# Hybrid encoder block: row differences tied behind a copy, fill drawn earlier, weight sums in other columns

## The chip, the cores and the metric

The kernel runs on one core of a Trainium2 chip. The metric is device time in microseconds (us) of one execution, lower is better; the median of several runs is compared. A core has five engines that work side by side, each on its own queue in order: TensorE (PE in the profile; PEld is its weight load), VectorE (DVE), ScalarE (ACT), GpSimd (POOL) and SyncE (SP), which here issues nearly all DMA transfers. SBUF is the on-chip memory of 128 partitions, PSUM the accumulators that TensorE writes.

## The reference, cut to what matters

One layer of a streaming encoder, 1024 tokens of width 1024, float32. A normalised input is projected once; three mixers work on parts of the projection, their outputs are projected, gated and summed, and a gated MLP with a short convolution follows.

```python
u = rms_norm(x, norm_mix_g) @ w_in                   # parts for MLA, FoX, SSD, gates
y_a = mla_branch(u_mla, ...) @ w_br_mla              # 8 heads, chunk-causal softmax
y_b = fox_branch(u_fox, ...) @ w_br_fox              # 8 heads, softmax with decay
y_c = ssm_branch(u_ssm, ...) @ w_br_ssm              # conv, SSD scan, gated norm
g = sigmoid(u_gate + b_gate)
x = x + (g[0] * y_a + g[1] * y_b + g[2] * y_c) @ w_out
x = x + conv_ffn(rms_norm(x, norm_ffn_g), ...)       # silu(gate) * val, then @ ffn_w_down
# inside the SSD scan, per chunk
decay = where(causal, exp(a_cum[i] - a_cum[j]), 0)   # per head
cb = C @ B.T
y_diag = (cb * decay) @ xdt
states = B.T @ (decay_to_end * xdt);  y_off = C @ h_in * exp(a_cum)
```

## The kernel before, in words

Every float32 product is computed as three products of a high and a low part (`split`: ScalarE copies the high part, VectorE subtracts it to get the low part), in tiles of 128 by 128 by 512. The stages, in order: projections for MLA and FoX, then attention, then the SSD scan, then the three branch projections (FoX, MLA, SSM), the output projection, and the MLP.

**Fill.** The columns of `w_in` for the scan's convolution (12 blocks) and the gates (24 blocks) need nothing but the normalised input. They are not computed in a stage of their own but dealt out as fill: `all_fill` is a generator that issues a block's 48 matrix multiplies (two halves of 24) and yields after every `grain` triples, with a booked cost of 0.65 us a triple. `grain` is 2 in attention (steps of 6 multiplies) and 4 in the scan (steps of 12). Results that other engines have to take out of PSUM are scheduled behind it by a simulated clock, `later(us, fn)`.

**merge.** TensorE's order in attention and scan is written out by `merge(streams, fill_us)`. It gets generators, each with a booked cost, and always advances the one whose share of its cost is smallest. `fill_us` is the cost that the fill may spend in this call; what is not spent stays owed to the next call. In attention a unit is a pair of query tiles of one head, four units a head, 16 heads; unit n issues its scores (`cost_s`) beside the value products of unit n-2 (`cost_v`), with fill worth `FILL_ATT` (1.08) times their cost. For n < 2 there are no value products yet. Ahead of the scan stands `merge([], 6.0)`, fill alone; the scan's ten turns get `FILL_SSD`, 11.3 us in eight turns, 12.0 in the ninth and 24.5 in the tenth, or what is left of the fill.

**Scan.** A chunk of the kernel's scan is a tile of 128 tokens (c = 0 to 7). Turn c runs `ssd_a` of chunk c, `ssd_b` of c-1 and `ssd_c` of c-2. `ssd_a` transposes the inputs into PSUM (L1506, tag `tp`, two slots; copied by L1507), transposes B and multiplies C with B into another `tp` tile (L1517, L1519), and splits B's transposes: ScalarE's copy `bTh`, VectorE's `bTl`, then VectorE multiplies the product with the causal mask (`cbm`, L1522). For each quarter of four heads ScalarE forms row differences of the cumulated decays with Relu (L1538, four instructions of 128 by 128), one exponential (L1539), and VectorE multiplies with `cbm` (L1540) to `E`. `ssd_b` adds states, the diagonal products `py` from `E` (L1574) and the products with the incoming state, scales by the gate, squares, takes a root on POOL and scales the result on ScalarE (L1601, kept in `scaled`). `ssd_c` transposes it (L1609) and copies it (L1610) for the store `ys_d`.

**Branches.** For each branch b the operand is loaded (`ar`), split (`ah`, `al`), and for eight columns j a weight tile and a gate tile are loaded, the weight split, and `ybr` computed (L1729); `out_half` (L1666 to L1673) multiplies with the gate and sums. The first two FoX operands are loaded during the scan; their split is tied behind `scaled` of the last chunk. The last gate block's activation is tied behind the second operand's copy.

**Weight sums.** The MLP's down projection uses sums of quarters of its weight. `down_sums` takes one of 11 row blocks: it first issues the stores of the previous set (`down_flush`), then two loads of 512 KB, four POOL additions (L939 to L942), and leaves two stores of 512 KB for the next flush. Six sets are formed during the projections, five in the branch stage, in tiles that the branch stage also uses for the first FoX operands and, from column 4 of the second branch, for four operands of the third (`early_raw`).

**What sets the order.** TensorE's instructions stay in the order written inside `tc.manual_schedule`. The other queues are ordered when the program is built, by a scheduler that simulates the program and issues what is ready. Two things bind it: `keep_in_program_order` puts an instruction behind the one traced before it on its engine (the loads and stores of `down_sums` are so bound), and `behind_(a, b)` puts a behind b on the same engine:

```python
def behind_(ins, other):
    tc.add_manual_dep(ins.ins, other.ins.name,
                      mybir.DependencyInfo(mybir.DependencyClass.NoSync, ...))
    return ins
```

It is an order in the queue only, without a semaphore.

Of the kernel before, what the change touches and what calls it, by code (L numbers as in the profile page):

```python
# [15 lines left out]
AF = mybir.ActivationFunctionType  # L16
# [26 lines left out]
def block_kernel(ctx: ExitStack, tc: tile.TileContext, x, positions, norm_mix_g, w_in, b_gate,  # L43
# [1380 lines left out]
    with ExitStack() as pt__:  # L1424
        atp = pt__.enter_context(TP("atp", 2))
        psp = pt__.enter_context(TP("psa", 1, space=PSUM))
        a_pm = Ring(atp, [P, S], F32, "pm", 6)
        a_nmx, a_rs = (Ring(atp, [P, 4], F32, n, 4) for n in ("nmx", "rs"))
        a_th, a_tl = (Ring(atp, [P, 512], F32R, n, PVLAG + 2) for n in ("pth", "ptl"))
        a_o1 = Ring(atp, [64, 256], F32, "o1", 1)  # L1430
        a_o2 = Ring(atp, [64, 256], F32, "o2", 4)
        a_s = Ring(psp, [P, 512], F32, "s", 3)
        a_tp = Ring(psp, [P, 512], F32, "tp", 2)
        o_acc = psp.tile([P, 2, 256], F32, name="o", tag="o")
        with tc.manual_schedule(engines={mybir.EngineType.PE}):
            names = [(br, h) for br in range(2) for h in range(8)]
            merge([], 5.0)
            units = [(n, jp) for n in range(16) for jp in range(4)]
            heads = {0: load_head(atp, *names[0])}
            load_values(atp, heads[0])  # L1440
            done = []
            for n in range(len(units) + 2):
                st, share = [], 0.0
                if n < len(units):
                    hn_, jp = units[n]
                    if jp == 0 and hn_ + 1 < 16:
                        heads[hn_ + 1] = load_head(atp, *names[hn_ + 1])
                    if jp == 3 and hn_ + 1 < 16:
                        load_values(atp, heads[hn_ + 1])
                    pn = []  # L1450
                    done.append((heads[hn_], jp, pn))
                    share += cost_s(jp)
                    st.append((scores(heads[hn_], jp, pn), cost_s(jp, len(heads[hn_].passes))))
                if n >= 2:
                    share += cost_v(done[n - 2][1])
                    me = []
                    me.append(values(*done[n - 2], me))
                    tp_next[:] = me
                    st.append((me[0], cost_v(done[n - 2][1])))
                merge(st, FILL_ATT * share)  # L1460
            flush()
            while pend:
                run_pv()
                clk[0] += 0.44
                run_until(clk[0])
            run_until(clk[0] + 3.0)
# [7 lines left out]
    with ExitStack() as ps__:  # L1474
# [22 lines left out]
        def ssd_a(o, c):  # L1497

            if c + 1 < NT:
                load_bc(obj[c + 1], c + 1)  # L1500
                load_rows(obj[c + 1], c + 1)
            xT = pool.tile([P, D], F32, name=uid("xT"), tag="xT", bufs=1)
            for g in range(2):
                pt = psp.tile([P, 512], F32, name=uid("stp"), tag="tp", bufs=2)
                for j in range(4):
                    T.transpose(pt[:, j * P:j * P + P], o.xs[:, 4 * g + j, :], ident)  # L1506
                A.activation(xT[:, 512 * g:512 * g + 512], pt, AF.Copy)  # L1507
                yield 0.44
            yield 0.0
            if c + 1 < NT:  # L1510
                load_xs(obj[c + 1], c + 1)
            o.bT = [pool.tile([P, 2, P], F32R, name=uid(n), tag=n) for n in ("bTh", "bTl")]
            o.c_ = [pool.tile([P, 2, P], F32R, name=uid(n), tag=n) for n in ("Ch", "Cl")]
            cbm = pool.tile([P, 2, P], F32, name=uid("cbm"), tag="cbm")
            pt = psp.tile([P, 4, P], F32, name=uid("stp"), tag="tp", bufs=2)
            for g in range(2):
                T.transpose(pt[:, g, :], o.bc[:, g, :], ident)  # L1517
            for g in range(2):
                T.matmul(pt[:, 2 + g, :], o.bc[:, g, :], o.bc[:, 2 + g, :], start=True, stop=True)  # L1519
            split(*o.bT, pt[:, 0:2, :])  # L1520
            split(*o.c_, o.bc[:, 2:4, :])
            V.tensor_mul(cbm, pt[:, 2:4, :], tri.unsqueeze(1).to_broadcast([P, 2, P]))  # L1522
            xv = xT.rearrange("p (h d) -> p h d", d=64)
            o.xd = pool.tile([P, 16, 64], F32, name=uid("xd"), tag="xd")
            V.tensor_mul(o.xd, xv, hb(dt, c))
            o.xdd = [pool.tile([P, 16, 64], F32R, name=uid(n), tag=n, bufs=1) for n in ("xddh", "xddl")]
            xdd = pool.tile([P, 16, 64], F32, name=uid("xdd"), tag="xdd", bufs=1)
            if c + 1 < NT:
                G.tensor_mul(xdd, xv, hb(dend, c))
            o.y = pool.tile([P, 16, 64], F32, name=uid("y"), tag="y", bufs=3)  # L1530
            G.tensor_mul(o.y, xv, Db.unsqueeze(2).to_broadcast([P, 16, 64]))
            yield 0.65
            o.E = []
            for q in range(4):
                E = pool.tile([P, 4, P], F32, name=uid("E"), tag="E", bufs=4)
                for hh in range(4):
                    h = 4 * q + hh
                    A.activation(E[:, hh, :], o.row[:, h, :], AF.Relu, scale=-1.0, bias=cumc[:, c, h:h + 1])  # L1538
                A.activation(E, E, AF.Exp, scale=-1.0)  # L1539
                V.tensor_mul(E, E, cbm[:, q // 2:q // 2 + 1, :].to_broadcast([P, 4, P]))  # L1540
                o.E.append(E)
                if q == 1 and c + 1 < NT:
                    split(*o.xdd, xdd)
                yield 0.0
# [71 lines left out]
        with tc.manual_schedule(engines={mybir.EngineType.PE}):  # L1616
            obj = {c: Head() for c in range(NT)}
            load_bc(obj[0], 0)
            load_xs(obj[0], 0)
            load_rows(obj[0], 0)  # L1620
            merge([], 6.0)
            grain[0] = 4
            for c in range(NT + 2):
                st = []
                if c < NT:
                    st.append((ssd_a(obj[c], c), 1.6))
                if 0 <= c - 2 < NT:
                    st.append((ssd_c(obj[c - 2], c - 2), *((0.88, 0.6) if c <= NT else (8.0, 0.2))))
                if 0 <= c - 1 < NT:
                    st.append((ssd_b(obj[c - 1], c - 1, obj.get(c - 2)), 6.4, 0.05))  # L1630
                merge(st, FILL_SSD[c])
            for _ in range(4):
                if advance(fill) is None:
                    break
# [3 lines left out]
    with ExitStack() as pe_:  # L1638
# [39 lines left out]
        for b, wsrc, nk in ((1, w_br_fox, 4), (0, w_br_mla, 4), (2, w_br_ssm, 8)):  # L1678
# [26 lines left out]
                al.append(l)  # L1705
            wv = wsrc[0].rearrange("(k p) c -> p k c", p=P)
            for j in range(NK):
                if (b, j) in ((1, 4), (0, 0), (2, 1), (2, 3), (2, 5)):
                    down_sums(ws_tiles())
                elif (b, j) in ((0, 3), (2, 6)):  # L1710
                    down_flush()
                if (b, j) == (0, 4):
                    early_raw = [t.rearrange("p a s -> p (a s)") for t in ws_tiles()]
                    for k in range(4):
                        SY.dma_start(early_raw[k], ys_d[k])
                if b == 0 and j >= 4:
                    early.append(ssm_operand(j - 4, early_raw[j - 4]))
                wh, wl = load_w(fpl, wv[:, :, j * P:j * P + P], nk, (scaled, gate_behind)[j][0] if b == 1 and j < 2 else None)
                g = fpl.tile([P, S], F32, name=uid("gl"), tag="t4", bufs=4)
                SY.dma_start(g, g_d[b][j])  # L1720
                pss = [psp.tile([P, 512], F32, name=uid("ybr"), tag="half") for half in range(2)]
                parts = [(half, 0, nk) for half in range(2)]
                if j == 0:
                    parts = [(half, k, k + 1) for k in range(nk) for half in range(2)]
                for half, k0, k1 in parts:
                    hs = slice(512 * half, 512 * half + 512)
                    for k in range(k0, k1):
                        for i, (w_, a_) in enumerate(((wh, ah), (wh, al), (wl, ah))):
                            T.matmul(pss[half], w_[:, k, :], a_[k][:, hs], start=k == 0 and i == 0,  # L1729
                                     stop=k == nk - 1 and i == 2)  # L1730
                    if k1 == nk:
                        out_half(b, j, half, g, pss[half])
# [481 lines left out]
```

## Time and profile before

| | us |
|---|---|
| median of 3 runs | 2002.59 |
| lowest, highest | 2002.17, 2005.0 |
| profiled execution, its own time | 2003.73 |
| its span | 2002.0 |

| stretch of the span (us) | stage |
|---|---|
| 0 to 384 | projections, MLA and FoX heads |
| 384 to 902 | attention with fill |
| 903 to 1094 | scan with fill |
| 1094 to 1270 | branches: FoX to about 1138, MLA to about 1182, SSM |
| 1270 to 1363 | output projection |
| 1363 to 2002 | MLP |

How to read the rows: a row of a timeline has the start in us from the span's start, the length, engine, line, instruction, output and inputs, and in brackets the time that the engine sat idle before it and what released it. "issue" means that the profile shows no releaser. A row of waits has the engine and line that waited, what it waited for, total us, times and longest. A row of a window has the stretch, its length, the busy time of PE, PEld, DVE, ACT and POOL with the number of instructions, TensorE's granted clock (1.00 is full), the DMA engines' busy share and GB/s; a window of one line only has PE and PEld.

### The profile page before, as it was taken

To read this page: it belongs to the slowest core of one execution; us is meant where nothing else is said; L and a number is where in the kernel's file an instruction comes from. 1 tells how busy PE (TensorE), PEld (TensorE's weight loads), DVE (VectorE), ACT (ScalarE), POOL (GpSimd) and SP (SyncE) were. 2 spreads that over 40 slices of the span, in tenths; PEclk is the share of its full clock that TensorE was granted. 3 is DMA by queue.
4 is the path that set the end of the run, shared out by engine and by line. 5 is a ranking of instruction groups with operands and counts; after the bars stand their busy time and mean duration, and the time that the engine had idled before them with its cause. 6 is when DMAs were issued, how large, how long until landed. Compare 5 with 4: busy or idle time off the path is not lost.

```text
span 2002.0 us, 28702 instructions
## 1 busy us (share of the span) xinstructions
PE 1977.5 (99%) x10185; PEld 1676.7 (84%) x10185; DVE 1365.9 (68%) x2345; ACT 944.5 (47%) x1778; POOL 651.9 (33%) x636
## 2 busy tenths in 40 slices
PE   8999999999999999999999999999999999999998
PEld 7989888888888888888888888888888888888887
DVE  7777567267666677656885476568997777666665
ACT  5555323255555556557775132225454444544432
POOL 5133322021212223213331252100764544423764
PEclk9999999999999999999999999999999999999999
DMA  5166857543535444427654786433332211249575
GB/s 178 52 195 210 277 179 224 165 125 105 139 114 145 122 120 133 125 78 238 183 192 139 259 284 202 144 119 107 104 95 90 78 55 53 78 159 337 188 262 185
DMA packets 278265, 312.18 MB, mean 156 GB/s; under 512 B 19197, under 2 KB 209289, under 8 KB 278122
## 3 DMA queue, kind: packets, MB, share of 16 engines
q1 hardware_dynamic: 278120, 310.35, 49.6%
q8 instruction: 80, 1.31, 0.3%
q14 instruction: 63, 0.52, 0.1%
q10 hardware_dynamic: 2, 0.00, 0.0%
HBM read 217.17 MB, written 93.13 MB: 155 GB/s over the span
## 4 chain that ended last, share of the span: by engine, by line
PE 86%; DVE 4%; issue 3%; DMA 3%; POOL 2%; ACT 2%; SPq 1%; ACTq 0%; DVEq 0%; POOLq 0%
PE mm L1179 19%; PE fx L798 9%; PE dn L2161 8%; PE ybr L1729 7%; PE ua L1820 6%; PE uc L1820 5%; PE ud L1820 4%; PE wo L1865 4%; PE s L1296 4%; PE tp L1384 3%; PE ub L1820 2%; PE fxv L188 2%; PE py L1574 1%; PE o L1357 1%; PE ckv L517 1%
## 5 line engine op out<-in xcount | busy, mean ns | idle before, releaser
L1326 POOL TENSOR_SCALAR pm<-pm,rs 128x128 f32<-128x128 f32 (+7 forms) x128 | 105.3, 826 | 413.9 <-DVE rs L1325 290.1
L1179 PE MATMUL mm<-hnh,wh 128*128 128x512 f32 x576 | 236.9, 411 | 0.0
L1179 PE MATMUL mm<-hnh,wl 128*128 128x512 f32 x576 | 226.0, 392 | 0.0
L1179 PE MATMUL mm<-hnl,wh 128*128 128x512 f32 x576 | 225.8, 392 | 0.0
L2161 PE MATMUL dn<-dr,dr 128*128 128x512 f32 x592 | 182.3, 389 | 0.0
L1319 ACT ACTIVATE pm<-s,nmx 128x128 f32<-128x128 f32 (+2 forms) x192 | 110.4, 581 | 64.9 <-DVE nmx L1314 61.4
L2161 PEld LDWEIGHTS dn<-dr,dr 128*128 128x128 f32 x592 | 111.1, 188 | 23.0
L1179 PEld LDWEIGHTS mm<-hnh,wl 128*128 128x128 f32 x576 | 108.1, 188 | 24.6
L1179 PEld LDWEIGHTS mm<-hnl,wh 128*128 128x128 f32 x576 | 108.9, 189 | 15.6
L1179 PEld LDWEIGHTS mm<-hnh,wh 128*128 128x128 f32 x576 | 108.8, 189 | 15.5
L1390 DVE TENSOR_TENSOR ptl<-tp,pth 128x512 fp32r<-128x512 f32 (+1 forms) x160 | 98.4, 633 | 32.8 <-ACT pth L1389 30.7
L1389 ACT ACTIVATE pth<-tp 128x512 fp32r<-128x512 f32 (+1 forms) x160 | 84.8, 555 | 72.6 <-PE tp L1384 72.5
L2161 PE MATMUL dn<-dr 128*128 128x512 f32 x296 | 115.3, 389 | 1.1 <-DVE dY L2178 1.1
L135 DVE TENSOR_TENSOR dr<-dr,dr 128x1024 fp32r<-128x1024 f32 x52 | 75.8, 1465 | 49.1 <-ACT dr L134 47.2
L1729 PE MATMUL ybr<-ah,wl 128*128 128x512 f32 x256 | 99.7, 390 | 1.1 <-DVE wl L135 1.1
L1729 PE MATMUL ybr<-al,wh 128*128 128x512 f32 x256 | 99.8, 390 | 0.0
L1729 PE MATMUL ybr<-ah,wh 128*128 128x512 f32 x256 | 99.7, 389 | 0.0
L134 ACT ACTIVATE dr<-dr 128x1024 fp32r<-128x1024 f32 x52 | 55.1, 1061 | 73.0 <-PE dn L2161 50.0
L1312 DVE TENSOR_REDUCE nmx<-s 128x1 f32<-128x384 f32 (+3 forms) x128 | 65.8, 518 | 32.7 <-PE s L1296 19.1
L134 ACT ACTIVATE wh<-wr 128x1024 fp32r<-128x1024 f32 (+1 forms) x40 | 35.1, 877 | 98.1 <-PE ybr L1729 45.9
L1384 PE MATMUL tp<-ident,pm 128*128 128x128 f32 x576 | 79.8, 273 | 0.6 <-POOL pm L1326 0.6
L135 DVE TENSOR_TENSOR wl<-S,wh 128x1024 fp32r<-128x1024 f32 x42 | 63.2, 1504 | 23.3 <-ACT wh L134 23.3
(531 smaller groups left out, 5782.7 us busy)
## 6 DMA issues: line engine op xcount, KB each, us to landing
dr<-act_d SPq DMA_DIRECT2D x99, 256.0 KB
wr<-in_w_in_dram SPq DMA_DIRECT2D x36, 512.0 KB
g_d<-t SPq DMA_DIRECT2D x24, 512.0 KB
gl<-g_d SPq DMA_DIRECT2D x24, 512.0 KB
wr<-in_ffn_w_up_dram SPq DMA_DIRECT2D x23, 512.0 KB
ws<-in_ffn_w_down_dram SPq DMA_DIRECT2D x22, 512.0 KB
wsum_d<-ws SPq DMA_DIRECT2D x22, 512.0 KB
act_d<-fa SPq DMA_DIRECT2D x22, 512.0 KB
```

The source lines that it names most:

```text
L134: i = A.activation(h, src, AF.Copy) if he is A else he.tensor_copy(h, src)
L135: return i, le.tensor_sub(l, src, f32(h))
L798: T.matmul(p, a(k), b(k), start=k == 0 and i == 0, stop=k == NK - 1 and i == 2)
L1179: T.matmul(ps, a[:, k, :], b[half][:, k, :], start=(k == 0 and i == 0), stop=(k == NK - 1 and i == 2))
L1319: pss[cj][1][0] = later(t0 + 0.9 + 0.1 * cj, lambda cj=cj, a_=a_, b_=b_: A.activation(p_[:, a_:b_], pss[cj][0][:, :b_ - a_], AF.Exp, bias= ...
L1326: G.tensor_scalar(p_[:, 0:n * P], p_[:, 0:n * P], rs[:, 3:4], 0.0, op0=ALU.mult, op1=ALU.add)
L1384: T.transpose(pt[:, off:off + P], pn[qi][0][:, k * P:k * P + P], ident)
L1389: later(cs + 0.05, lambda th=th, pt=pt, off=off: A.activation(th[:, :off], pt[:, :off], AF.Copy))
L1390: pl[0] = later(cs + 0.6, lambda th=th, tl=tl, pt=pt, off=off: V.tensor_sub(tl[:, :off], pt[:, :off], f32(th[:, :off])))
L1729: T.matmul(pss[half], w_[:, k, :], a_[k][:, hs], start=k == 0 and i == 0, stop=k == nk - 1 and i == 2)
L1820: T.matmul(ps, a, b, start=first and n == 0, stop=n == 11, skip_group_check=not first)
L2161: T.matmul(ps[m], a[:, ts_], b[:, 512:], start=first_ and j == 0 and q == 0, stop=j == NFH - 1 and q == 2, skip_group_check=not first_)
```

## The change

Four edits. The first two units of attention draw 2.0 us more of fill each. The fill ahead of the scan is 9.0 us instead of 6.0. All 16 row differences of a scan chunk are tied on ScalarE behind the copy of that chunk's transposed B. The first set of weight sums in the branch stage moves from column 4 to column 2 of the FoX branch, the second from column 0 of the MLA branch to column 6 of the FoX branch, and the flush of the second set's stores from column 3 to column 2 of the MLA branch; the last three sets stay.

```diff
@@ attention, for n in range(len(units) + 2)
-                merge(st, FILL_ATT * share)
+                merge(st, FILL_ATT * share + (2.0 if n < 2 else 0.0))
@@ ssd_a
-            split(*o.bT, pt[:, 0:2, :])
+            b_copy, _ = split(*o.bT, pt[:, 0:2, :])
...
-                    A.activation(E[:, hh, :], o.row[:, h, :], AF.Relu, scale=-1.0, bias=cumc[:, c, h:h + 1])
+                    behind_(A.activation(E[:, hh, :], o.row[:, h, :], AF.Relu, scale=-1.0, bias=cumc[:, c, h:h + 1]),
+                            b_copy)
@@ ahead of the scan
-            merge([], 6.0)
+            merge([], 9.0)
             grain[0] = 4
@@ branches, for j in range(NK)
-                if (b, j) in ((1, 4), (0, 0), (2, 1), (2, 3), (2, 5)):
+                if (b, j) in ((1, 2), (1, 6), (2, 1), (2, 3), (2, 5)):
                     down_sums(ws_tiles())
-                elif (b, j) in ((0, 3), (2, 6)):
+                elif (b, j) in ((0, 2), (2, 6)):
                     down_flush()
```

## The prediction

> **What bounds the kernel now.** I read the page first, then TensorE's waits stage by stage, then the timelines of all engines around each wait. First the page: its head and the line of busy time.
>
> ```profile
> span 2002.0 us, 28702 instructions
> PE 1977.5 (99%) x10185; PEld 1676.7 (84%) x10185; DVE 1365.9 (68%) x2345; ACT 944.5 (47%) x1778; POOL 651.9 (33%) x636
> ```
>
> TensorE is busy for 1977.5 of 2002.0 us. The diff takes no matrix multiply away; it only changes their order and what runs beside them. So it can win only idle time of TensorE in the stages that it touches, and it can lose wherever it uncovers a latency. The waits of TensorE in attention and at its end are few (microseconds in total, times, longest):
>
> ```profile
> PE o L1349 <- DVE o L1367: 1.6, 1, 1.6
> PE stp L1506 <- DVE o L1367: 0.9, 1, 0.9
> PE s L1296 <- ACT pm L1319: 0.8, 1, 0.8
> PE tp L1384 <- POOL pm L1326: 0.6, 1, 0.6
> ```
>
> In the branch products there is one:
>
> ```profile
> PE ybr L1729 <- DVE wl L135: 1.1, 1, 1.1
> ```
>
> And in the scan three waits, as TensorE's timeline shows them (start, length, instruction, in brackets the idle time before it):
>
> ```profile
> 955.94 0.63 PE L1506 MATMUL stp<-ident,t 128*128 128x128 f32 x4 [1.16 <-issue]
> 999.11 0.63 PE L1506 MATMUL stp<-ident,t 128*128 128x128 f32 x4 [0.79 <-PE py L1574]
> 1020.34 0.63 PE L1506 MATMUL stp<-ident,t 128*128 128x128 f32 x4 [1.38 <-issue]
> ```
>
> That is 0.8 + 0.6 in the first heads, 0.9 where the scan's first transposes wait for attention's last PSUM read, 3.33 in the scan, 1.1 in the second branch: 6.7 us that the edits aim at. The 1.6 lies in the middle of attention, where no edit is. 0.2% of this kernel, about what a measurement of it can tell from no change, is 4 us.
>
> **The change, part by part.** *Fill at the start of attention.* No instruction is added. Two units draw 2.0 us more each from the fill, and the 1.4 us of waits above come a few units later. Their late partners are a score row's maximum and a normalisation, which the first convolution block's vector work holds up; that block now ends a unit sooner in program order, so its taps meet shorter score rows. Ends: -1.4 (both gone) and +1.6 (the shifted phase makes another wait like the row of 1.6). I take half of the gain, -0.7.
>
> *Fill before the scan, 9.0 for 6.0.* Twelve more multiplies (one step at the grain of the fill) can stand under the 0.9 us wait. Ends -0.9 and 0; 2.7 us of work over a wait of 0.9 is ample, so -0.9.
>
> *What both draws take from the end.* The fill is finite: 36 blocks of 48 multiplies, booked at 0.65 us for three, 374.4 us in all. Before, 5.0 are drawn first, 1.08 x 16 x 14.48 = 250.2 in attention (the two cost functions give 0.74 + 1.22 + 1.86 + 2.50 and 0.72 + 1.60 + 2.48 + 3.36 for a head's four units, 14.48 together), 6.0 before the scan and 11.3 x 8 + 12.0 in its first nine turns: 363.6. The tenth turn, which asks for 24.5, gets what is left, 10.8, in steps of twelve multiplies 48. The trace agrees: the 72 multiplies after the scan's last diagonal product are 24 of turn nine and 48 of turn ten.
>
> ```profile
> 1076.20:1094.00 17.80, 17.22 (x72) 13.13 (x72) 1.00 0.59 192
> ```
>
> After, 370.6 are drawn by then and 3.8 are left, one step of 12. So 36 multiplies that stood at the scan's end go earlier, and chunk 7's output chain loses its cover. TensorE's rows are transposes of chunk 6, twice of chunk 7, and the second branch multiply:
>
> ```profile
> 1081.70 0.60 PE L1609 MATMUL stp<-ident,y 128*128 128x128 f32 x4
> 1087.63 0.60 PE L1609 MATMUL stp<-ident,y 128*128 128x128 f32 x4
> 1090.85 0.60 PE L1609 MATMUL stp<-ident,y 128*128 128x128 f32 x4
> 1094.34 0.50 PE L1729 MATMUL ybr<-al,wh 128*128 128x512 f32 x1
> ```
>
> ScalarE's are the scaling of chunk 7, the second copy of its transposes and the first branch operands:
>
> ```profile
> 1082.96 1.15 ACT L1601 ACTIVATE y<-y,yr 128x1024 f32<-128x1024 f32 x1
> 1091.48 0.60 ACT L1610 ACTIVATE yT<-stp 128x512 f32<-128x512 f32 x1 [2.48 <-PE stp L1609]
> 1091.98 2.00 ACT L134 ACTIVATE ah<-ar 128x1024 fp32r<-128x1024 f32 x2
> ```
>
> Count from chunk 6's last transposes (1081.70 = 0). Four transposes and 12 multiplies take 1090.85 - 1087.63 = 3.22 us. By the row of 72 twelve multiplies are 12 x 17.22/72 = 2.87, so four transposes 0.35. After the change chunk 7's transposes start at 3.22 and, with nothing between, at 3.57; TensorE is free at 3.92. The scaling is done at 2.41 (1082.96 + 1.15), so the transposes do not wait. The second copy starts 0.63 after its transposes (1091.48 - 1090.85) and the first branch operand 0.50 after that: 4.70. Its low half lets the second branch multiply start 2.36 later (1094.34 - 1091.98): 7.06. One multiply (0.24) falls into the gap, so TensorE idles 7.06 - 0.24 - 3.92 = 2.9 us where it idled nothing. Ends: +1.0, if the operand's copy goes right behind the scaling (a little behind 2.41 instead of 4.70, with the first weights' copy between), and +3.5, if one more copy as long as the 0.60 of the row above slips in. I take +2.9, since the order in the rows above has the operand behind both copies.
>
> *The row differences behind the copy of B's transposes.* No instruction and no semaphore is added; 16 activations per chunk go behind one copy on ScalarE's queue, and behind them wait four exponentials, VectorE's four products, and TensorE's diagonal products. The three waits of 3.33 us are for the two-slot PSUM ring: the next chunk's transposes need the slot of B's transposes, which VectorE's mask product reads last. Chunk 2, then chunk 5:
>
> ```profile
> 949.25 0.61 PE L1519 MATMUL stp<-bc 128*128 128x128 f32 x4
> 944.34 1.26 ACT L1538 ACTIVATE E<-row,strict 128x128 f32<-128x128 f32 x4
> 945.51 0.58 ACT L1507 ACTIVATE xT<-stp 128x512 f32<-128x512 f32 x1
> 951.84 0.37 ACT L134 ACTIVATE bTh<-stp 128x256 fp32r<-128x256 f32 x1
> 955.43 0.41 DVE L1522 TENSOR_TENSOR cbm<-stp,tri 128x256 f32<-128x256 f32 x1
> 963.27 1.00 PE L1574 MATMUL py<-xd,E 128*128 128x64 f32 x8
> ...
> 992.77 0.61 PE L1519 MATMUL stp<-bc 128*128 128x128 f32 x4
> 993.49 0.37 ACT L134 ACTIVATE bTh<-stp 128x256 fp32r<-128x256 f32 x1
> 998.59 0.41 DVE L1522 TENSOR_TENSOR cbm<-stp,tri 128x256 f32<-128x256 f32 x1
> ```
>
> In chunk 2 B's copy comes 2.0 us after its transposes end at 949.86, and row differences at 944.34 push the copy that feeds VectorE to 945.51: with them gone both come over 1 us sooner, and the 1.16 us wait goes. In chunk 5 the copy is already prompt, and VectorE comes to the mask product only 5 us later; the tie helps there only if VectorE's order changes too. So I count the first wait whole and the other two by half: -(1.16 + 1.08) = -2.25. Ends: -3.33, and a loss from this side: between B's transposes and the first diagonal product ScalarE and VectorE have this much to do (window, span, then busy time of PE, PEld, DVE, ACT, POOL):
>
> ```profile
> 949.90:963.30 13.40, 12.24 (x67) 10.31 (x66) 12.91 (x19) 9.65 (x21) 2.81 (x4) 1.00 0.67 195
> L1538 ACT ACTIVATE E<-row,strict 128x128 f32<-128x128 f32 x112 | 35.7, 390 | 11.6 <-PE py L1574 11.3
> L1539 ACT ACTIVATE E<-E 128x512 f32<-128x512 f32 x28 | 17.1, 621 | 0.2
> ```
>
> Half of a chunk's row differences and exponentials ran before the copy and now come into this window: 8 x 35.7/112 + 2 x 17.1/28 = 3.8 us, so ScalarE has 13.4 us of work in 13.4 us. Only the first quarter is due at 963.27, so I take no loss, but 1 us in each of seven chunks, +7, is the upper end.
>
> *Weight sums in columns 2 and 6 of the first branch.* The same instructions: per sum two loads and two stores of 512 KB on SP and four POOL operations; the second set moves from the second branch's start to the first branch's column 6, its stores from column 3 to column 2 of the second branch. SP in the second branch now:
>
> ```profile
> 1134.90 0.86 SPq L945 DMA_DIRECT2D wsum_d<-ws  x2
> 1135.80 2.54 SPq L937 DMA_DIRECT2D ws<-in_ffn_w_down_dram  x2
> ```
>
> The DMA share (behind the clock, the number after the last bracket) in a window of each branch:
>
> ```profile
> 1115.00:1120.00 5.00, 5.00 (x24) 4.14 (x23) 1.98 (x3) 0.63 (x1) 0.00 (x0) 1.00 0.49 139
> ...
> 1140.00:1145.00 5.00, 5.00 (x24) 4.14 (x23) 2.39 (x3) 0.45 (x1) 1.22 (x1) 1.00 1.02 397
> ```
>
> Those four transfers are 2 MB, 5.3 us at 397 GB/s, ahead of the gates and weights of the second branch in a saturated stretch; the 1.1 us wait for a weight's low half follows it. At column 6 the DMA engines are half idle. Behind the stores on SP stand that column's weight and gate loads, which may wait for POOL's sums a few us; the half idle transfers cover that. Column 2 instead of 4 moves little: the first loads still stand behind a gate load that waits for the last fill block's store. Ends -1.1 and +1.1 (the same wait in another column); I take -1.1.
>
> **Sum:** -0.7 - 0.9 + 2.9 - 2.25 - 1.1 = -2.05 us. The profiled execution took 2003.73 us for its span of 2002.0, 1.14 above the median of the runs, 2002.59. From the median: 2000.5 us.
>
> **Rivals.** *Faster:* the branch operand's copy is put right behind the scaling. For it: its data is loaded long before. Against: the order now. With all other waits gone the sum is -1.4 - 0.9 - 3.33 - 1.1 + 1.0 = -5.7: 1996.9.
> *Slower:* the products of the row differences reach TensorE late in the scan. For it: 13.4 us of ScalarE work in 13.4 us, VectorE 12.91 busy there. Against: only a quarter is due first. At 1 us in seven chunks: -0.7 - 0.9 + 2.9 + 7 - 1.1 = +7.2, 2009.8; it passes +4 us from 0.55 us a chunk.
> *The tie does nothing:* VectorE's own queue holds the mask product in all chunks, as in chunk 5. The 3.33 stay: +0.2, 2002.8.
> *The clock falls:* the gap at the scan's end lets TensorE's clock drop, and the branch's first multiplies run at half pace for a stretch as long as the gap, 2.9 us, and lose half of it, 1.45: 2002.0. Against it stands the longest wait of the kernel, with the granted clock (the number behind the five engines) of the window in which it ended:
>
> ```profile
> PE tp L509 <- DVE hnl L235: 2.8, 1, 2.8
> ...
> 38.00:42.00 4.00, 2.36 (x14) 2.12 (x15) 3.97 (x15) 1.65 (x5) 3.45 (x8) 1.00 0.42 129
> ```
>
> The clock stayed at 1.00 after 2.8 us of idleness. [...]
>
> **Chances.** My sum 0.37 (its own range 1998.8 to 2003.4: the scan's term between its lower end and the first wait alone, attention's between -1.4 and nothing, the branch's between -1.1 and nothing), faster rival 0.29, tie without effect 0.11, clock 0.04, slower rival 0.19. So faster by over 0.2% 0.32 (the rival and the forecast's lower edge), slower 0.19, within 0.49. The range goes from 1995.9, the faster rival without the 1.0 that it still pays, to 2007.0, the slower rival at 0.6 us a chunk; above that lies most of the slower rival, below little.
>
> **What the next profile shows.** Right: 12 instead of 48 multiplies after chunk 6's last transposes, then a wait of about 2 and one of about 1 us before the first two branch products; no wait of the scan's first transposes on attention's sums; waits of the chunk transposes under 1.2 us together; no row difference of a chunk before its B copy; weight sums on POOL wholly inside the first branch and no wait in the second. Wrong: a wait of the diagonal products for E in every chunk, or no gap before the branch products.

## The result, and the profile after

The changed kernel is slower: 2014.84 us median of six runs (2011.7 to 2018.19) against 2002.38 for the kernel before in the same session (2000.77 to 2005.0); the ratio is 1.0059, 95% interval 1.0045 to 1.0072. The forecast was 2000.5, its range ended at 2007.0. Line numbers after L1538 are higher by one in the changed kernel, so L1507 is the same line in both and L1566 is the old L1565. The page's head and busy line:

```profile
span 2013.2 us, 28698 instructions
PE 1983.8 (99%) x10185; PEld 1683.8 (84%) x10185; DVE 1362.4 (68%) x2345; ACT 943.0 (47%) x1778; POOL 659.8 (33%) x636
```

The same 10185 multiplies, but TensorE is busy 6.3 us longer, beside some 5 us more of waits. The larger entries among its waits (us in total, times, longest), in the scan and the branches:

```profile
PE pof L1549 <- DVE hst L1567: 3.7, 1, 3.7
PE stp L1610 <- ACT y L1602: 3.6, 1, 3.6
PE ybr L1730 <- ACT ah L134: 2.4, 1, 2.4
PE ybr L1730 <- DVE wl L135: 2.2, 2, 1.4
PE stp L1506 <- issue: 1.0, 1, 1.0
```

The longer busy time goes with the clock. Three windows of the changed kernel (the number after the five engines and their counts is the granted clock):

```profile
950.00:960.00 10.00, 6.29 (x28) 5.13 (x27) 10.00 (x10) 3.66 (x6) 4.21 (x2) 0.87 0.42 126
980.00:990.00 10.00, 7.43 (x32) 6.55 (x32) 6.16 (x10) 5.86 (x15) 1.23 (x2) 0.66 0.09 27
1100.00:1110.00 10.00, 6.86 (x23) 5.18 (x22) 5.32 (x5) 5.96 (x8) 0.00 (x0) 0.83 0.65 222
```

Six windows of 10 us stand below 1.00 here, from 0.66 to 0.96; in the kernel before none does. A mean of 0.87 over 10 us costs 1.3 us; with 0.96 in the window behind it 1.7; 0.66 costs 3.4, 0.83 costs 1.7. "Half clock" stands for what windows of 1 us show inside these drops: 0.50 in each of the six from 982 to 988 us, and 0.54, 0.50, 0.50 and 0.76 from 1104 to 1108. These prices are of one execution each: the six executions of the changed kernel have mean clocks from 0.995 to 0.998.

Where the 11.2 us of span went, from the first instructions of each stage (before, after): scan's first transposes 903.5 and 907.1; first branch product 1094.1 and 1102.5; output projection 1270.0 and 1282.1; end 2002.0 and 2013.2. Thirty-six fill multiplies left the scan's end; thirty of them now stand ahead of the scan and six inside it. The thirty are, at 0.228 us from start to start, 6.8 us of work that has only changed place. So:

| stretch | span, us | without the moved fill |
|---|---|---|
| to the scan's first transposes | +3.6 | -3.2 (1.0 lost at the start, where nothing was edited; 4.2 won in attention and at its end) |
| scan to the first branch product | +4.8 | +11.6 |
| branches | +3.7 | +3.7 (of it 2.5 still the scan's end: 0.8 of wait, 1.7 of half clock) |
| the rest | -0.9 | -0.9 |

Most of the 1.0 us at the start is the clock too. The loss arises before 245 us, at the place of the prediction's longest wait, whose 2.8 us had left the clock at 1.00: the changed kernel waits 1.97 us there, 0.9 less, and then loses 1.7 us at 0.96 and 0.87 in two windows (rows in the last section).

**The wait of 3.7 us.** The names in the rows: `pst` is the PSUM tile with one half of a chunk's new states, `hst` the running state, which VectorE first decays and then sums with `pst`; `pof` is the product with the incoming state; `xd` (VectorE), `xdd` and `y` (GpSimd) are products of a chunk's transposed inputs `xT`. VectorE, GpSimd and TensorE in the scan, changed kernel:

```profile
950.78 2.40 DVE L1566 TENSOR_TENSOR hst<-hst,cdec 128x512 f32<-128x512 f32 x1
953.10 2.92 DVE L1525 TENSOR_TENSOR xd<-xT,dt 128x1024 f32<-128x1024 f32 x1
955.94 0.67 DVE L1567 TENSOR_TENSOR hst<-hst,pst 128x512 f32<-128x512 f32 x1
950.72 1.91 POOL L1529 TENSOR_TENSOR xdd<-xT,dend 128x1024 f32<-128x1024 f32 x1 [2.33 <-ACT xT L1507]
952.58 2.35 POOL L1531 TENSOR_TENSOR y<-xT,Db 128x1024 f32<-128x1024 f32 x1
956.76 0.47 PE L1549 MATMUL pof<-hsh,Ch 128*128 128x512 f32 x1 [3.71 <-DVE hst L1567]
```

The second `pof` needs the PSUM slot of the second `pst`, which the second state sum (955.94) frees. That sum now stands on VectorE's queue behind the next chunk's `xd`. Both operations ahead of it are also drawn out: the state's decay takes 2.40 us here and 0.68 at its shortest, `xd` 2.92 and 1.21, each beside a product of GpSimd that started ahead of it (950.72 and 952.58; more in the last section). In the kernel before, VectorE did both state sums at 939.5 to 942.4, ahead of `xd` and of GpSimd's products; the second sum and the next `xd` there:

```profile
941.69 0.69 DVE L1566 TENSOR_TENSOR hst<-hst,pst 128x512 f32<-128x512 f32 x1
946.12 1.23 DVE L1525 TENSOR_TENSOR xd<-xT,dt 128x1024 f32<-128x1024 f32 x1 [0.84 <-ACT xT L1507]
```

**The wait of 3.6 us.** GpSimd, then ScalarE and TensorE:

```profile
974.65 2.91 POOL L1529 TENSOR_TENSOR xdd<-xT,dend 128x1024 f32<-128x1024 f32 x1
977.55 0.26 POOL L180 TENSOR_SCALAR yr<-rg_t,yr 128x1 f32<-128x1 f32 x1
977.77 1.90 POOL L1531 TENSOR_TENSOR y<-xT,Db 128x1024 f32<-128x1024 f32 x1
979.66 1.31 POOL L179 TENSOR_SCALAR rg_t<-yr,rg_v 128x1 f32<-128x1 f32 x1
981.07 0.27 POOL L180 TENSOR_SCALAR yr<-rg_t,yr 128x1 f32<-128x1 f32 x1
981.37 1.15 ACT L1602 ACTIVATE y<-y,yr 128x1024 f32<-128x1024 f32 x1 [1.25 <-POOL yr L180]
982.57 1.11 PE L1610 MATMUL stp<-ident,y 128*128 128x128 f32 x4 [3.62 <-ACT y L1602]
```

The next chunk's two products stand inside the root (L179 and L180) of the chunk that TensorE is to transpose: 4.8 us in the middle of a chain of small steps. In the kernel before each root ran through; the last step of one, and the product behind it:

```profile
965.16 0.26 POOL L180 TENSOR_SCALAR yr<-rg_t,yr 128x1 f32<-128x1 f32 x1
966.15 1.91 POOL L1529 TENSOR_TENSOR xdd<-xT,dend 128x1024 f32<-128x1024 f32 x1 [0.72 <-ACT xT L1507]
```

**The scan's end.** TensorE and ScalarE:

```profile
1099.08 1.04 PE L1610 MATMUL stp<-ident,y 128*128 128x128 f32 x8
1102.50 0.50 PE L1730 MATMUL ybr<-ah,wh 128*128 128x512 f32 x1 [2.38 <-ACT ah L134]
1103.76 0.55 PE L1730 MATMUL ybr<-al,wh 128*128 128x512 f32 x1 [0.76 <-DVE al L135]
1100.41 1.08 ACT L1611 ACTIVATE yT<-stp 128x512 f32<-128x512 f32 x2 [1.77 <-DMA ys_d<-yT]
1101.39 2.00 ACT L134 ACTIVATE ah<-ar 128x1024 fp32r<-128x1024 f32 x2
```

Twelve multiplies stand between the last transposes of chunks 6 (1095.86) and 7 (1099.08), as worked out, and the gaps are 2.4 and 0.8 us. What held the copies was the store of chunk 6 from the one tile `yT`.

### The profile page after: what moved, and what is told of

It reads as the page before. It is cut to its first block, busy times and chain, and to the rows that moved or that the text cites. A ratio compares the mean times of both kernels' runs of the same rounds, so it can differ in the third digit from the quotient of the medians.

```text
span 2013.2 us, 28698 instructions
## 1 busy us (share of the span) xinstructions
PE 1983.8 (99%) x10185; PEld 1683.8 (84%) x10185; DVE 1362.4 (68%) x2345; ACT 943.0 (47%) x1778; POOL 659.8 (33%) x636
## 4 chain that ended last, share of the span: by engine, by line
PE 45%; DVE 2%; issue 2%; POOL 1%; DMA 1%; ACT 1%; SPq 0%; ACTq 0%; POOLq 0%; DVEq 0%
PE dn L2162 10%; PE ybr L1730 7%; PE ua L1821 6%; PE uc L1821 5%; PE ud L1821 4%; PE wo L1866 4%; PE mm L1179 3%; PE ub L1821 2%; PE py L1575 1%; DVE wl L135 0%; DMA ar<-att_d 0%; DMA wsum_d<-ws 0%; PE pof L1549 0%; PE pt L1773 0%; PE stp L1610 0%
```

## The experiments

First theory: the tie makes the row differences late, and the scan's two waits come from it. First rival: the moved fill makes them.

**Each part alone, and all without the tie.** Edits: `tie_alone` has only the `behind_(..., b_copy)` lines, `fill_alone` only the 2.0 and the 9.0, `sums_alone` only the columns, `no_tie` the last two together.

> Only the tie of the row differences to the copy of B's transposes. Theory (the tie): the changed kernel lost some 8 us in the scan, in two waits of 3.7 and 3.6 us and in the half clock behind them, because the tied row differences come late and VectorE and GpSimd then work in another order; the tie alone brings waits of that size too, 2 to 8 us slower than before (2004 to 2010). Rival (the fill): the scan's waits come from the fill that was moved ahead of it, so the tie alone shows none over 2 us and its 3.3 us of transposes' waits go: 1999 to 2001.

> Both larger draws of fill, nothing else. Theory (the tie): no wait over 2 us inside the scan; attention and its end gain 4 us as they did in the changed kernel, the scan's end loses 3.1 us of idle time and 1.7 us of half clock, as there: 2003, plus or minus 2. Rival (the fill): the scan shows its two waits over 3 us here too, and the time is 2008 to 2012.

> Only the weight sums in other columns. Both theories: the scan as before. The changed kernel had 2.2 us of waits for weights' low halves in the branches where 1.1 stood before: 2003 to 2004 if that is the moved sums' doing, 2001.5 if my step of -1.1 us held when nothing else moves.

> The changed kernel without the tie. Theory (the tie): the scan's two waits over 3 us are gone, the gap at the scan's end stays: 2003 to 2005. Rival (the fill): 2010 to 2014, as with the tie.

| run | median, us | ratio to before, 95% interval |
|---|---|---|
| tie_alone | 2010.18 | 1.0039 (1.0025 to 1.0052) |
| fill_alone | 2006.08 | 1.0014 (1.0005 to 1.0023) |
| sums_alone | 2001.47 | 0.9993 (0.9984 to 1.0002) |
| no_tie | 2006.88 | 1.0025 (1.0015 to 1.0034) |

The tie alone costs 7.8 us, 0.2 more than its band allowed; fill and sums together 4.5, 1.9 us above the band expected for them. Without the tie neither of the scan's waits over 3 us is there; the longest of `fill_alone` and `no_tie` in the scan is 2.1 us, for a load, where none over 2 was expected. The waits of `tie_alone`, and VectorE's row that now stands ahead of the second state sum:

```profile
PE pof L1549 <- DVE hst L1567: 5.2, 2, 4.2
PE stp L1506 <- issue: 2.9, 2, 1.8
950.54 2.27 DVE L135 TENSOR_TENSOR xddl<-xdd,xddh 128x1024 fp32r<-128x1024 f32 x1 [0.57 <-ACT xddh L134]
```

Here not `xd` but a split that waits for ScalarE and GpSimd stands there. The transposes' waits, at which the tie aims, are still 2.9 us. So the tie brings the loss, as the theory says. The fill alone is 1 us above its expected band. Its trace has the two gaps at the scan's end, 2.4 and 0.8 us with the clock at 0.83 behind them, but it is of the fastest of its eleven executions (2002.06 us); what the other ten lose beyond that, 2 to 6 us, no trace shows. Seven of them have a mean clock of 0.997, the profiled one 0.999.

**Late row differences, or the order of the queues?** A finer pair: either the late row differences hold up all that follows, or the tie only tips the build's scheduler into two bad orders. Edits on the changed kernel:

```diff
@@ state_first
-            V.tensor_mul(o.xd, xv, hb(dt, c))
+            xd_ = V.tensor_mul(o.xd, xv, hb(dt, c))
+            if state_[0] is not None:
+                behind_(xd_, state_[0])        # state_[0]: the latest second state sum
@@ root_first
-                G.tensor_mul(xdd, xv, hb(dend, c))
+                xdd_ = G.tensor_mul(xdd, xv, hb(dend, c))
+                if root_[0] is not None:
+                    behind_(xdd_, root_[0])    # root_[0]: the last step of the earlier root; y likewise
@@ own_tile (on fill_alone)
+            if c == NT - 1:
+                o.yT = pool.tile([P, D], F32, name=uid("xT"), tag="xT", bufs=1).rearrange(...)
```

`both_first` has the first two.

> The changed kernel, with VectorE's product xd of the next chunk put behind the second state sum. Theory (queue order): TensorE's wait of 3.7 us, for the PSUM slot that the second state sum frees, and the 1.7 us that its half clock costs go: 2009 to 2010. Rival (late row differences: all that follows ScalarE's late burst is late, whatever the order): the wait moves to the diagonal products or to the scaling of the chunk and the time stays at 2013 to 2016.

> The changed kernel, with GpSimd's two products of a chunk put behind the last step of the earlier chunk's root. Theory (queue order): TensorE's wait of 3.6 us for the scaled chunk, and the 3.4 us that the half clock behind it costs, go: 2007 to 2009. Rival (late row differences): the products, now later, hold up the state sums instead; 2013 to 2016.

> Both orders put right, the tie still in. Theory (queue order): the scan has no wait over 2 us and no half clock, only the scan's end loses: 2002 to 2005. Rival (late row differences): at least one wait over 2 us stays in the scan and the time is over 2009.

> Both larger draws of fill alone (median 2006.1), with the transposes of chunk 7 copied to a tile of their own, so that they need not wait until chunk 6's are stored. Theory: ScalarE's copies stood 1.8 us for that store, and the branch operand behind them; the first branch multiply comes about 2 us sooner and the clock stays up, 3 to 4 us: 2002 to 2004. Rival: the operand's copy comes that late in any case (its place on ScalarE's queue, or its load): no change, 2005 to 2007.

| run | median, us | ratio to before, 95% interval |
|---|---|---|
| state_first | 2009.99 | 1.0034 (1.0021 to 1.0046) |
| root_first | 2007.80 | 1.0023 (1.0014 to 1.0033) |
| both_first | 2003.65 | 1.0005 (0.9996 to 1.0014) |
| own_tile | 2004.21 | 1.0005 (0.9997 to 1.0014) |

Against the changed kernel's median that is -4.9, -7.0 and -11.2 us (the kernel before stood between 2002.4 and 2003.6 in the sessions), with 16 row differences a chunk still tied. Each of the first two leaves the other's wait in place: `state_first` still has 3.8 us for the scaled chunk, `root_first` 3.7 us for the PSUM slot. The two largest of the scan's waits in `both_first`:

```profile
PE stp L1509 <- issue: 1.2, 1, 1.2
PE pof L1558 <- DVE hst L1576: 1.0, 1, 1.0
```

The order of the queues is the cause; the late row differences as such cost nothing that shows. The two prices hold the clock as well, and not only behind the wait in question: the trace of `root_first` has no drop in the scan or at its end, not even behind its wait of 3.7 us. `own_tile` took the store's wait away, yet TensorE's first wait fell only from 2.4 to 1.7 us: copies and operand follow the transposes in line in any case. Its 1.9 us against `fill_alone` lie inside overlapping intervals; this run settles little.

**Even turns.** If the fill of a turn decides which order the scheduler finds, the number of multiplies per turn should do it without any new tie. The arithmetic of `merge` gives 60, 48, 48, 60, 48, 48, 60, 48 in the changed kernel's first eight turns; 10.4 us gives 48 in each, and 48 instead of 12 in the tenth:

```diff
-    FILL_SSD = [11.3] * 8 + [12.0, 24.5]
+    FILL_SSD = [10.4] * 8 + [12.0, 24.5]
```

`even_fill` is that on the changed kernel, `even_no_tie` the same without the tie, `even_alone` that line on the kernel before. `orders_no_sums` is `both_first` with the weight sums in their old columns.

> The changed kernel, all four edits, with 10.4 for 11.3 us of fill in the scan's first eight turns: 48 multiplies in every turn instead of 60, 48, 48, 60, ..., and 48 instead of 12 left for the end. Theory (the draws, tie and fill together, put the other engines' queues into a bad order, and the scan's end lacks cover): no wait over 2 us in the scan, none before the first branch product, 1998 to 2001. Rival (the tied row differences are late in themselves): with less fill in three of the turns the scan waits for them, 2005 or more.

> The same without the tie: 10.4 us of fill a turn, both larger draws, the moved sums. Theory: the end's cover is back, and no wait over 2 us, 1998 to 2001; what the tie is worth is the difference to the kernel with it: 3 us if it takes the transposes' waits away as I forecast, 0 if an even order does that already.

> The kernel with both orders put right (median 2003.7), without the moved weight sums. That kernel had 2.8 us of waits for weights' low halves in the branches; the moved sums alone, on the kernel before, had none. If the moved sums make them in this company, they go here and the time is 2000.5 to 2002; if the scan's shorter end makes them, they stay: 2003 to 2004.5.

> The kernel before with 10.4 for 11.3 alone: none of the four edits, 84 instead of 48 multiplies at the end. The waits of attention and at its end (1.6 and 0.9 us) stay: 2000 to 2003. If it is as fast as the kernel with all edits, the even turns make the gain and not the edits.

| run | median, us | ratio to before, 95% interval |
|---|---|---|
| even_fill | 1999.89 | 0.9983 (0.9975 to 0.9992) |
| even_no_tie | 2021.32 | 1.0089 (1.0075 to 1.0102) |
| orders_no_sums | 2001.87 | 0.9991 (0.9982 to 1.0) |
| even_alone | 2003.22 | 0.9999 (0.999 to 1.0008) |

All four edits with even turns are 3.7 us faster than the kernel before; the same without the tie is 18 us slower. I had expected 1998 to 2001 for both: for `even_no_tie` that was far off. The transposes' waits of `even_no_tie`, with ScalarE, then a wait of TensorE and ScalarE in `even_fill`:

```profile
PE stp L1506 <- issue: 10.5, 5, 2.5
PE stp L1506 <- DMA t<-xbc_d: 4.9, 1, 4.9
973.26 1.15 ACT L1601 ACTIVATE y<-y,yr 128x1024 f32<-128x1024 f32 x1 [3.59 <-POOL yr L180]
974.31 1.26 ACT L1538 ACTIVATE E<-row,strict 128x128 f32<-128x128 f32 x4
975.48 0.58 ACT L1507 ACTIVATE xT<-stp 128x512 f32<-128x512 f32 x1
```

```profile
977.01 0.63 PE L1506 MATMUL stp<-ident,t 128*128 128x128 f32 x4 [0.55 <-PE stp L1610]
985.82 0.60 ACT L1507 ACTIVATE xT<-stp 128x512 f32<-128x512 f32 x1 [3.49 <-PE stp L1506]
987.26 1.14 ACT L1602 ACTIVATE y<-y,yr 128x1024 f32<-128x1024 f32 x1
```

Without the tie four row differences (1.26 us) stand ahead of the copy that feeds VectorE, in nearly every chunk, and the next chunk's transposes wait 1.8 to 2.5 us for the mask product. With the tie the copy comes first and those waits are 0.55, four times, and once 1.6. In three of the five chunks the wait without the tie is 1.83 to 1.85 us, 1.3 more than 0.55, about the length of the four row differences. That is the mechanism that the prediction gave to the tie. It accounts for 6.7 of the 21.4 us between the two kernels. The 4.9 us for a load is a wait of another kind; what makes that load late was not tried. Another 6.8 us are a longer busy time of TensorE, whose clock stood at 0.66 to 0.95 in five windows of the scan without the tie. Even turns alone change nothing that the runs can tell (2003.22 is 0.2 us above the expected band).

**The two questions left.** `even_no_sums` is `even_fill` with the old columns; `even_tie_alone` is the kernel before with the tie and 10.4, whose first turn holds 42 multiplies.

> The kernel of all four edits with even turns (median 1999.9, 3.0 us of waits for weights' low halves in the branches), without the moved weight sums. If the sums make those waits: they fall to about the 1.1 us of the kernel before, 1997 to 1998.5. If the larger draws or the tie make them: they stay, 1999.5 to 2001.

> The kernel before with the tie and 10.4 for 11.3 us a turn, nothing else. Its first turn holds 42 multiplies for 48; VectorE's queue has the next chunk's xd ahead of the second state sum again in four chunks, and GpSimd's two products stand inside a root once, as in the changed kernel. Theory (queue order): a wait of over 3 us for a PSUM slot or a scaled chunk is back, 2006 to 2012. Rival (it is the number of multiplies per turn): no such wait, and only attention's 2.5 us above the kernel with all edits: 2001 to 2004.

`even_no_sums`: 1997.96 us, ratio 0.9976 (0.9965 to 0.9987), the fastest kernel of this study. `even_tie_alone`: 2013.88, ratio 1.0048 (1.0034 to 1.0062), 1.9 us above the band of the theory, and both waits are back. The first two lines are its waits, the rest are VectorE and TensorE of `even_fill` in the MLA branch:

```profile
PE stp L1610 <- ACT y L1602: 4.0, 1, 4.0
PE pof L1549 <- DVE hst L1567: 3.7, 1, 3.7
```

```profile
1138.97 1.28 DVE L1660 SCALAR_TENSOR_TENSOR al<-ws,pc_n,ah 128x1024 fp32r<-128x1024 f32 x1
1140.17 0.68 DVE L135 TENSOR_TENSOR wl<-wr,wh 128x512 fp32r<-128x512 f32 x1
1140.90 0.50 PE L1730 MATMUL ybr<-ah,wl 128*128 128x512 f32 x1 [1.46 <-DVE wl L135]
```

So the same tie, with the same 48 multiplies in the later turns, wins or loses by the order that the other queues get. And in the company of the other edits the moved sums do cost: their tiles come free sooner, the SSM branch's early operands are loaded and split sooner (the first of these loads is issued at 1114.4 us, with the old columns at 1142.4), and that split (`al`) stands on VectorE ahead of the weight's low half on which TensorE waits, here 1.46 us and at 1153.66, in the same order, 1.58. With the old columns both waits are gone, one of 0.8 us for a weight's high half is there, and the time falls by 1.9 us (by the ratios 0.0007, 1.4 us). The intervals of the two ratios overlap, so the waits are shown and the size of the gain is not.

## Why the prediction was wrong, point by point

- *Fill at the start of attention and before the scan.* Right in sign, too small: -1.6 forecast together, -4.2 measured. The 0.9 went as said, and the 1.6 us wait in the middle of attention, where the prediction said that no edit is, fell to 0.2. These and 0.2 at the two early waits are some 2.5 us; the other 1.7 stand in no wait of the lists, and where they lie was not traced.
- *What both draws take from the end.* Twelve multiplies left, gaps of 2 and 1 us: 2.4 and 0.8 measured, 3.1 against 2.9. The sum came out close in part by luck: a store held the copies, so that the operand's copy came 0.8 us later than told (5.53 us after chunk 6's transposes for 4.70), and TensorE's own rows ahead of and inside the gap are 0.6 us longer than counted. What failed is the chance of the falling clock, 0.04: behind this gap the clock stood at 0.83 over 10 us, at half for 3.4 of them by the windows of 1 us, and 1.7 us more were lost. That chance rested on one execution, in which a wait of 2.8 us had left the clock at 1.00; at the same place the changed kernel waits 1.97 us and the clock falls, to 0.87 in the window behind it. That the stretch at half pace is as long as the gap was the author's estimate and is not what the trace shows: 3.4 us here behind gaps of 3.1, 6.8 behind the wait of 3.6.
- *The tie.* This is the step that failed: -2.25 forecast, and alone it cost 7.8. Its mechanism exists, as the even turns show (transposes' waits of 10.5 us in five chunks down to 3.8), but alone the tie took only 0.4 of the 3.3 us away (2.9 are left in `tie_alone`). Wrong was the tacit assumption that the other queues would keep their order. They are ordered anew at each build; the tie changed two places, each with a price that the prediction did not have: 4.9 us for the state sums, 7.0 for the root, differences in the clock included.
- *The slower rival* had the sign and, at 2009.8 us, a good part of the size, but another mechanism: there is no wait of the diagonal products for `E` in the trace, and none of the signs of "wrong" that the prediction named came up; of those of "right", the twelve multiplies, the gaps behind them, the free start of the scan and under 1.2 us for the chunk transposes all held, beside a loss of 12 us. Only the sign on the weight sums failed: TensorE waits 2.2 us in the second branch. The signs looked only where the edits aimed, and so could not tell this loss from a gain. What it called the tight engine, ScalarE, was not late where it mattered; VectorE's and GpSimd's order was.
- *Weight sums.* -1.1 forecast; alone -0.9 with an interval that holds zero, in company +1.4 to +2.8. The old wait went, as said; that the freed tiles let other loads and splits start sooner, ahead of what TensorE waits for, was missing from the step.
- *The range.* Its upper end, 2007.0, came from a price per chunk that the trace did not show. A bound for a step that makes a scheduler order four queues anew should have held single gaps of the size of a displaced operation, 3 to 4 us, and for each the 1.7 to 3.4 us that the clock cost behind such gaps in the changed kernel.

## What to carry to other kernels

Where a build-time scheduler orders the queues, a tie or a changed amount of fill is not a local edit: it draws a new order for every queue, so price it by the order that comes out, and bind what matters (here two ties, the state sums ahead of the next chunk's `xd` and the root ahead of GpSimd's next products, were worth 11 us). The same amount of fill per turn makes an order repeat in every turn, a good one (3.7 us won with the tie) or a bad one (18 us lost without it), so look at the order before taking it over. When a buffer or tile comes free earlier, ask which load and which split it lets in, and what they will stand in front of.

## What the runs showed of the hardware

*The clock falls after gaps that are alike only in part.* The wait of 3.71 us in the changed kernel left the clock at 0.87 and 0.96 in its windows. In `root_first` the same place has the same wait and a full clock:

```profile
956.75 0.47 PE L1556 MATMUL pof<-hsh,Ch 128*128 128x512 f32 x1 [3.71 <-DVE hst L1574]
950.00:960.00 10.00, 6.29 (x33) 4.99 (x32) 10.00 (x10) 4.20 (x9) 4.21 (x2) 1.00 0.41 127
```

And in `own_tile` two shorter waits with one multiply between them were enough:

```profile
1092.86 0.50 PE L1732 MATMUL ybr<-ah,wh 128*128 128x512 f32 x1 [1.68 <-ACT ah L134]
1094.12 0.80 PE L1732 MATMUL ybr<-al,wh 128*128 128x512 f32 x1 [0.76 <-DVE al L135]
1090.00:1100.00 10.00, 7.56 (x31) 5.77 (x30) 5.77 (x6) 5.96 (x8) 0.00 (x0) 0.83 0.72 232
```

Nor does the longer of two waits at one place make the drop. At the place of the prediction's longest wait, in a stage that no edit touches, 2.83 us left the clock at 1.00 in the kernel before; in the changed kernel 1.97 us did not:

```profile
38.71 1.29 PE L509 MATMUL tp<-ident,cn 128*128 128x128 f32 x5 [1.97 <-DVE hnl L235]
40.00:50.00 10.00, 10.00 (x61) 9.96 (x61) 7.80 (x27) 3.26 (x9) 8.52 (x20) 0.87 0.14 54
```

The two waits at the scan's end, 2.4 and 0.6 to 0.8 us, left 0.83 in the changed kernel, 1.00 in `root_first` and 0.66 in `both_first`. The windows of the last two:

```profile
1090.00:1100.00 10.00, 6.86 (x34) 5.30 (x33) 5.23 (x5) 7.50 (x10) 0.00 (x0) 1.00 0.55 184
1090.00:1100.00 10.00, 9.11 (x26) 6.87 (x27) 6.20 (x7) 4.61 (x7) 0.75 (x1) 0.66 0.76 278
```

So the length of the gap alone does not decide, and the same gap can cost 0, 1.7 or 3.4 us more than its length. It is not fixed by the kernel either: the profiled execution of `root_first` has a mean clock of 1.000, its ten others 0.997. One trace is one draw. What decides was not shown.

*VectorE's and GpSimd's products are longer beside each other.* In the rows of the 3.7 us wait, a state decay that takes 0.68 us at its shortest took 2.40 and ended 0.55 us after GpSimd's first product (952.63), and `xd`, 1.21 us at its shortest, ended 1.1 us after GpSimd's second (954.93). In the scan of the kernel before, the product that started second was the longer one. Three `xd` that started 0.05 us ahead of a product of GpSimd took 1.23 us and GpSimd's product 2.94. Five that started 0.05 to 0.62 us behind one took 2.36 to 2.94 us and ended 1.07 to 1.09 us after it; four of these five products took 1.91 us. Why was not shown.
